# A Winograd down-projection in fp32 on one core: four PSUM banks a unit instead of seven, input and weight tiles split in two, operand loads on another queue

## The chip, the core and the metric

The kernel runs on one NeuronCore of a Trainium2 chip. It is one launch that computes a whole encoder layer for two sequences. The metric is the device time of the launch in microseconds (us). Engines are named as the profile names them: PE (TensorE, matmuls), DVE (VectorE), ACT (ScalarE), POOL (GpSimd) and SP (SyncE, which here only issues DMAs). Each engine carries out its own instructions in the order in which they stand in its program, and waits where one of them needs something that another engine or a DMA has not finished.

## The reference, cut to what matters

```python
def encoder_layer(x, ...):                       # x: (1, L, 1024); L = 2048 ("s") and L = 512 ("p")
    ...                                          # three mixers side by side, output projection
    x = x + cat @ w_out
    h = rms_norm(x, norm2_g)
    u = dwconv3(h @ w_ffn_in, ffn_conv_w, ffn_conv_b)          # 1024 -> 2 * 2816, then a width-3 convolution
    act = jax.nn.gelu(u[..., :D_FF], approximate=False) * u[..., D_FF:]
    return x + act @ w_ffn_out                                 # 2816 -> 1024: the down-projection
```

Everything is fp32. The change concerns the last line, `x + act @ w_ffn_out`, and one queue in the line with `w_ffn_in`.

## The kernel before

Every product is formed from three matmuls (`mm3`, lines 326 to 328): an operand is split into a rounded part and a rest (`split`, ACT copies the rounded part on line 320, DVE or POOL subtracts it on line 321), and high x high, high x low and low x high are added up in one PSUM bank.

The layer runs in stages. The mixers and the first quarter of the up-projection take the first half of the span. Then `ffn_in7` computes the remaining up-projection as 2 x 2 blocks by Winograd's form of Strassen's scheme, with seven products instead of eight; its right-hand operands are seven sums of the transposed rows, prepared earlier in DRAM (`ops`) and fetched by `ffn_operands` (tiles `st`, loaded on line 1351; two buffers; split into the tiles `o`). It loads the up-projection's weights as tiles `fw` on SP's queue, and POOL forms their sums `fs` (lines 1398 to 1402). Its results, the activations, go to DRAM as `acts` and `actp`.

The last stage is the down-projection, `ffn_out`. It cuts the 2560 rows into ten units of 256 (eight of the long sequence, two of the short one) and the 2816 inner columns into eleven pairs of 128-blocks. Three passes take four, four and three pairs, and each pass goes over all ten units, adding its sum to a partial result that it loads from DRAM and stores again (`x2`, then `part0`, `part1`, then the output). For each unit and pair, four 128 x 128 blocks of activations (A11 to A22) and four 128 x 512 blocks of weights (B11 to B22) make one Winograd step with seven products:

- `out_weights` loads the pair's weights into `b` (line 1495, one buffer, 1 MB), forms four differences `t` on DVE (line 1500) and splits the seven operands into one tile `w` (five buffers: four pairs of a pass and one of the next).
- `out_input` loads a unit's four blocks into `a` (lines 1517 and 1518, two buffers, SP's queue), forms four sums on DVE (line 1521) and splits all seven operands with one instruction on ACT and one on DVE into one tile `ah` (three buffers).
- `ffn_out` adds each of the seven products up over the pass's pairs in a bank of its own, 21 matmuls a pair. A unit so holds seven of the eight banks, and the next unit begins in the eighth and goes on in banks as they are read. At a unit's end one ACT copy (line 1556: `p1`, tile `s0`) and seven DVE adds (line 1554) read the banks: `u2` (tile `s1`), `u3` (tile `s2`), and five adds into the four quarters of `x`. Four adds on POOL finish `x`, and POOL issues the store of `x` (line 1568) and the load of the next unit's `x` (line 1544). `x` has one buffer, so that load waits for the store.

At a unit's end the banks are combined like this:

```python
nc.scalar.activation(p1, ps[0], AF.Copy)
add(u2, ps[1], p1)
add(u3, ps[2], u2)
add(x12, ps[3], x12)
add(x22, ps[3], x22)
add(x11, ps[4], x11)
add(x21, ps[5], x21)
add(x12, ps[6], x12)
```

The order on each engine is not the order of the code: a scheduler places the instructions by its own estimate of when each can start, and tile buffers are reused as their last readers finish. What the engines carry out is therefore read from the built program.

## Time and profile before

| what | value |
|---|---|
| time, median of 3 runs | 3182.96 us (3179.11 to 3183.93) |
| the profiled execution's own time | 3188.23 us |
| its span, first to last instruction | 3186.5 us |
| mean granted PE clock | 0.973 |
| busy: PE, DVE, ACT, POOL | 2932.5, 2307.0, 1382.2, 810.8 us |
| down-projection, from the up-projection's last matmul to the end | 2495.8 to 3186.5 us |
| its matmuls | 3 x 770 |

The profile is one execution. A row of a group gives the line, engine, operation, output<-input, count, busy time and mean duration, then the idle time of the engine just before these instructions and what ended it. A row of the timeline gives start, duration and the instruction, with the wait before it in square brackets. A row of the waits gives who waited for whom, the total, how often and the longest. Busy matmuls overlap in this profile (each shows about 0.4 us where one is issued every 0.23 us), so PE's pace is read from counts. Line numbers are those of the kernel before.

### The profile page before, as it was taken

What the parts mean: (1) busy time and instruction counts of PE and PEld (TensorE: products, weight loads), DVE (VectorE), ACT (ScalarE), POOL (GpSimd) and SP (SyncE); (2) the same over time, 40 slices, a digit from 0 to 9 for tenths busy, and PEclk for the clock granted to TensorE, in tenths of its full rate; (3) what the DMA queues carried; (4) which work ended last, traced back from release to release, by engine and by line L of the source; (5) the groups of instructions that cost most, each with busy time, mean ns of one, the idle gap of its engine ahead of it and who ended that gap; (6) DMA issues with size and microseconds to landing.
All of it is one profiled execution on the core that took longest, in us unless ns stands there. A gap on an engine that the chain in (4) does not pass through costs nothing.

```text
span 3186.5 us, 41534 instructions
## 1 busy us (share of the span) xinstructions
PE 2932.5 (92%) x15134; PEld 2412.1 (76%) x15134; DVE 2307.0 (72%) x3792; ACT 1382.2 (43%) x2259; POOL 810.8 (25%) x626
## 2 busy tenths in 40 slices
PE   7999999999999989999789999899999798799887
PEld 6887888888888777777568888678888576577665
DVE  7443577769998768766478888877777777877775
ACT  5222444458876448543344444444444421321211
POOL 1000000012233231003154444433333033223243
PEclk9999999999999999999889999999999899899998
DMA  5555576653433465675642222322222343443444
GB/s 176 147 151 144 159 222 183 179 165 114 133 106 95 154 184 163 175 203 184 197 140 80 80 80 80 126 80 83 83 80 80 119 168 127 167 156 130 157 147 144
DMA packets 450338, 441.25 MB, mean 138 GB/s; under 512 B 76553, under 2 KB 380041, under 8 KB 447317
## 3 DMA queue, kind: packets, MB, share of 16 engines
q1 hardware_dynamic: 420709, 341.16, 36.5%
q0 software_dynamic: 19200, 73.41, 6.3%
q10 hardware_dynamic: 10224, 24.03, 1.9%
q8 instruction: 119, 1.95, 0.3%
q14 instruction: 86, 0.70, 0.1%
HBM read 313.73 MB, written 124.78 MB: 138 GB/s over the span
## 4 chain that ended last, share of the span: by engine, by line
PE 28%; DVE 9%; DMA 7%; POOL 3%; issue 2%; ACT 1%; SPq 0%; DVEq 0%; ACTq 0%; POOLq 0%
PE b L326 9%; PE b L328 9%; PE b L327 9%; DVE a L1521 3%; DVE ah L321 2%; DMA a<-acts 2%; DVE x L1554 2%; POOL x L1554 2%; DMA x<-part1s 1%; DMA out_dram<-x 1%; DVE w L321 1%; DMA a<-actp 1%; POOL o L321 1%; ACT ah L320 1%; DMA fw<-in_w_ffn_in_dram 1%
## 5 line engine op out<-in xcount | busy, mean ns | idle before, releaser
L326 PE MATMUL b<-o,fk 128*128 128x512 f32 x1056 | 423.6, 401 | 16.8 <-ACT fk L320 13.2
L327 PE MATMUL b<-o,fk 128*128 128x512 f32 x1056 | 417.1, 395 | 5.1 <-DVE o L321 4.2
L328 PE MATMUL b<-o,fk 128*128 128x512 f32 x1056 | 418.6, 396 | 2.7 <-DVE fk L321 2.7
L326 PE MATMUL b<-w,ah 128*128 128x512 f32 x770 | 320.5, 418 | 92.1 <-DVE s L1554 41.7
L327 PE MATMUL b<-w,ah 128*128 128x512 f32 x770 | 312.3, 406 | 0.7 <-DVE w L321 0.5
L328 PE MATMUL b<-w,ah 128*128 128x512 f32 x770 | 311.8, 406 | 0.4 <-DVE ah L321 0.4
L1446 DVE SCALAR_TENSOR_TENSOR cv<-u,cst,cv 128x1024 f32<-128x1024 f32 (+2 forms) x264 | 298.9, 1173 | 7.9 <-ACT cv L1444 3.8
L320 ACT ACTIVATE ah<-a 128x896 fp32r<-128x896 f32 x110 | 104.1, 951 | 425.1 <-DVE a L1521 392.9
L326 PEld LDWEIGHTS b<-w,ah 128*128 128x128 f32 x770 | 149.1, 194 | 159.1 <-DVE s L1554 58.7
L1554 POOL TENSOR_TENSOR x<-x,s 128x512 f32<-128x512 f32 x120 | 174.7, 1481 | 349.1 <-DVE x L1554 349.1
L1521 DVE TENSOR_TENSOR a<-a 128x128 f32<-128x128 f32 x440 | 176.8, 428 | 107.0 <-DMA a<-acts 76.1
L326 PEld LDWEIGHTS b<-o,fk 128*128 128x128 f32 x1056 | 199.6, 189 | 63.8 <-ACT fk L320 13.6
L328 PEld LDWEIGHTS b<-o,fk 128*128 128x128 f32 x1056 | 199.7, 189 | 55.6 <-DVE fk L321 3.9
L327 PEld LDWEIGHTS b<-o,fk 128*128 128x128 f32 x1056 | 199.9, 189 | 53.5 <-DVE o L321 4.6
L1409 DVE TENSOR_TENSOR u<-b,u 128x512 f32<-128x512 f32 x220 | 151.3, 688 | 122.2 <-PE b L328 119.9
L326 PE MATMUL b<-W,h 128*128 128x256 f32 (+1 forms) x672 | 225.3, 335 | 2.2 <-ACT W L320 0.9
L349 POOL TENSOR_TENSOR rr<-ss,mhalf 128x1 f32<-128x1 f32 x60 | 37.1, 618 | 746.5 <-DVE ss L347 709.8
L1398 POOL TENSOR_TENSOR fs<-fw 128x512 f32<-128x512 f32 x44 | 94.0, 2136 | 513.1 <-DMA fw<-in_w_ffn_in_dram 418.3
L327 PE MATMUL b<-W,h 128*128 128x256 f32 (+1 forms) x672 | 215.1, 320 | 0.7 <-DVE pu L973 0.3
L328 PE MATMUL b<-W,h 128*128 128x256 f32 (+1 forms) x672 | 214.0, 318 | 0.0
L326 PE MATMUL b<-h,W 128*128 128x256 f32 x640 | 200.2, 313 | 3.6 <-ACT W L320 1.7
L328 PE MATMUL b<-h,W 128*128 128x256 f32 x640 | 184.9, 289 | 3.7 <-DVE W L321 3.7
(249 smaller groups left out, 7366.4 us busy)
## 6 DMA issues: line engine op xcount, KB each, us to landing
fw<-in_w_ffn_in_dram SPq DMA_DIRECT2D x132, 512.0 KB, 3.9
a<-acts SPq DMA_DIRECT2D x176, 128.0 KB, 2.6
nx<-in_x_sample_dram SPq DMA_DIRECT2D x32, 512.0 KB, 4.5
tf<-in_t2f_s_dram SPq DMA_DIRECT2D x64, 256.0 KB, 3.7
ops<-o SPq DMA_DIRECT2D x8, 1792.0 KB, 8.7
st<-ops SPq DMA_DIRECT2D x14, 1024.0 KB, 5.4
raw<-in_w_in_dram SPq DMA_DIRECT2D x44, 256.0 KB, 3.0
acts<-cv ACTq DMA_DIRECT2D x22, 512.0 KB, 4.3
```

The source lines that it names most:

```text
L320: self.keep(nc.scalar.activation(hi, x, AF.Copy))
L321: self.keep((engine or nc.vector).tensor_tensor(lo, x, hi.bitcast(F32), op=ALU.subtract))
L326: nc.tensor.matmul(ps, lhsT=lhi, rhs=rhi, start=start, stop=False, skip_group_check=more)
L327: nc.tensor.matmul(ps, lhsT=lhi, rhs=rlo, start=False, stop=False, skip_group_check=more)
L328: nc.tensor.matmul(ps, lhsT=llo, rhs=rhi, start=False, stop=stop, skip_group_check=more)
L349: self.keep(nc.gpsimd.tensor_tensor(r[:n], ss[:n], self.mhalf[:n, 0:1], op=ALU.pow))
L1398: nc.gpsimd.tensor_tensor(s12[:, 0:4], a21, a22, op=ALU.add)
L1409: nc.vector.tensor_tensor(o, ps, x, op=ALU.add)
L1446: nc.vector.scalar_tensor_tensor(o, u[:, part, c + i - 1:c + i - 1 + k], self.fcw[:, i, m:m + 1], o, op0=ALU.mult, op1=ALU.add)
L1521: nc.vector.tensor_tensor(a[:, o], a[:, x], a[:, y], op=op)
L1554: engine.tensor_tensor(o, a, b, op=ALU.add)
```

## The change

Four of the seven products get a bank: `pa`, `pb`, `pd` and `pc`. They are formed pair by pair as before (12 matmuls a pair, "early" products). When all pairs of the unit are done, `pa` is copied, `pb` and `pd` are added into `u2` and `u3`, and `pc` is added into `x22`. Then `pa`, `pd` and `pc` are not started afresh: another product ("late" product, all pairs of the unit one after the other) is accumulated on top of what the bank holds, and the sum is added into `x11`, `x21` and `x12`. A unit holds four banks, two units all eight. One bank add on DVE and one add on POOL fall away in each unit.

The late products need their operands after the early ones of all pairs, so the tiles are cut in two: inputs `ah` (four operands, two buffers) and `ag` (three operands, five buffers), each with its own split; weights `w` (four operands, five buffers) and `v` (three operands, four buffers), with five splits a pair instead of four. `a` gets a third buffer. The next pass's weights are written in the code after the last late product of the last unit, no longer between its pairs. Apart from the down-projection, `ffn_operands` issues the seven `st` loads of its first call on POOL's queue; those of the second call stay on SP's.

```diff
-    def ffn_operands(self, pool, stage, src):
+    def ffn_operands(self, pool, stage, src, queue):
...
-                self.nc.sync.dma_start(out=x, in_=src[:, op])
+                queue.dma_start(out=x, in_=src[:, op])
...
     def out_weights(self, pool, stage, f0):
-        w = pool.tile([128, 2, 7, 512], F32R, tag="w", bufs=5, name="w")
...
+        w = pool.tile([128, 2, 4, 512], F32R, tag="w", bufs=5, name="w")
         self.split(b11, w[:, 0, 0], w[:, 1, 0])
         less(t[:, 0], b12, b11)
         less(t[:, 1], b22, t[:, 0])
-        self.split(t[:, 0:2], w[:, 0, 3:5], w[:, 1, 3:5])
         less(t[:, 2], t[:, 1], b11)
+        self.split(t[:, 1:3], w[:, 0, 2:4], w[:, 1, 2:4])
+        self.split(t[:, 0], w[:, 0, 1], w[:, 1, 1])
+        v = pool.tile([128, 2, 3, 512], F32R, tag="v", bufs=4, name="v")
         less(t[:, 3], b21, t[:, 1])
-        self.split(t[:, 2:4], w[:, 0, 5:7], w[:, 1, 5:7])
-        self.split(b[:, 1].rearrange("p (h d) -> p h d", h=2), w[:, 0, 1:3], w[:, 1, 1:3])
-        return w
+        self.split(b[:, 1].rearrange("p (h d) -> p h d", h=2), v[:, 0, 0:2], v[:, 1, 0:2])
+        self.split(t[:, 3], v[:, 0, 2], v[:, 1, 2])
+        return w, v
 
     def out_input(self, pool, n, r0, f0):
-        a = pool.tile([128, 8, 128], F32, tag="a", bufs=2, name="a")
+        a = pool.tile([128, 8, 128], F32, tag="a", bufs=3, name="a")
...
-        h = pool.tile([128, 2, 7, 128], F32R, tag="ah", bufs=3, name="ah")
-        self.split(a[:, 0:7], h[:, 0], h[:, 1])
-        return h
+        h = pool.tile([128, 2, 4, 128], F32R, tag="ah", bufs=2, name="ah")
+        g = pool.tile([128, 2, 3, 128], F32R, tag="ag", bufs=5, name="ag")
+        self.split(a[:, 0:4], h[:, 0], h[:, 1])
+        self.split(a[:, 4:7], g[:, 0], g[:, 1])
+        return h, g
...
-                ps = [bank() for _ in order]
+                pa, pb, pd, pc = (bank() for _ in range(4))
...
-                    for p, (ja, jb) in zip(ps, order):
-                        self.mm3(p, h[:, 0, ja], h[:, 1, ja], ws[k][:, 0, jb], ws[k][:, 1, jb], k == 0, k == len(fs) - 1)
-                    if u == len(units) - 1 and i + 1 < len(passes):
-                        for g in passes[i + 1][len(nxt):k + 2]:
-                            nxt.append(self.out_weights(pw, stage, g))
+                    w = ws[k][0]
+                    for p, ja, jb in ((pa, 0, 0), (pb, 2, 2), (pd, 3, 3), (pc, 1, 1)):
+                        self.mm3(p, h[:, 0, ja], h[:, 1, ja], w[:, 0, jb], w[:, 1, jb], k == 0, k == len(fs) - 1)
...
+                def late(p, ja, jb):
+                    for k, g in enumerate(gs):
+                        v = ws[k][1]
+                        self.mm3(p, g[:, 0, ja], g[:, 1, ja], v[:, 0, jb], v[:, 1, jb], False, k == len(gs) - 1, True)
+
+                nc.scalar.activation(p1, pa, AF.Copy)
+                add(u2, pb, p1)
+                add(u3, pd, u2)
+                add(x22, pc, x22)
+                late(pa, 1, 0)
+                add(x11, pa, x11)
+                late(pd, 2, 2)
+                add(x21, pd, x21)
+                late(pc, 0, 1)
+                if u == len(units) - 1:
+                    for g in ahead:
+                        nxt.append(self.out_weights(pw, stage, g))
+                add(x12, pc, x12)
                 add(x22, x22, u3, nc.gpsimd)
-                add(x11, x11, p1, nc.gpsimd)
-                add(x21, x21, u3, nc.gpsimd)
-                add(x12, x12, u2, nc.gpsimd)
+                for o in (x21, x12):
+                    add(o, o, u2, nc.gpsimd)
```

What stands on DVE in a steady unit of the first pass, before. `s1` and `s2` are `u2` and `u3`; `b0` to `b4` are banks; the three `a` and `ah` that follow belong to the next two units:

```order
L1554 TENSOR_TENSOR s2_22752<-b0_22619,s1_22751 128x512
L1554 TENSOR_TENSOR x_22665<-b1_22620,x_22665 128x512 x2
L1554 TENSOR_TENSOR x_22665<-b2_22621,x_22665 128x512
L1554 TENSOR_TENSOR x_22665<-b3_22622,x_22665 128x512
L1554 TENSOR_TENSOR x_22665<-b4_22623,x_22665 128x512
L321 TENSOR_TENSOR ah_22807<-a_22804,ah_22807 128x896
L1521 TENSOR_TENSOR a_22837<-a_22837 128x128 x4
L321 TENSOR_TENSOR ah_22840<-a_22837,ah_22840 128x896
```

And in the change, from the add of `pc` (bank `b3`) into `x22` on. `a_22828`, `a_22855` and `a_22880` are the second, third and fourth inputs of the next unit, `a_22959` is the first of the one after it:

```order
L1558 TENSOR_TENSOR x_22685<-b3_22646,x_22685 128x512
L1522 TENSOR_TENSOR a_22880<-a_22880 128x128 x4
L1558 TENSOR_TENSOR x_22685<-b0_22643,x_22685 128x512
L1558 TENSOR_TENSOR x_22685<-b2_22645,x_22685 128x512
L321 TENSOR_TENSOR ag_22836<-a_22828,ag_22836 128x384
L321 TENSOR_TENSOR ag_22863<-a_22855,ag_22863 128x384
L321 TENSOR_TENSOR ag_22888<-a_22880,ag_22888 128x384
L1558 TENSOR_TENSOR x_22685<-b3_22646,x_22685 128x512
L1522 TENSOR_TENSOR a_22959<-a_22959 128x128 x4
L321 TENSOR_TENSOR ag_22967<-a_22959,ag_22967 128x384
L321 TENSOR_TENSOR ah_22862<-a_22855,ah_22862 128x512
```

The bank adds no longer stand together: input sums and splits stand between them, and the `ah` split of the next unit's third input comes after the sums of an input one unit later.

What stands on DVE at the end of the first pass, before. `w_23714` belongs to the second pair of the next pass (its differences stand far ahead of here), `b_23764` to the third:

```order
L321 TENSOR_TENSOR w_23714<-b_23715,w_23714 128x512
L1521 TENSOR_TENSOR a_23880<-a_23880 128x128
L321 TENSOR_TENSOR w_23714<-t_23717,w_23714 128x1024 x2
L321 TENSOR_TENSOR w_23714<-b_23715,w_23714 128x1024
L321 TENSOR_TENSOR ah_23829<-a_23826,ah_23829 128x896
L1521 TENSOR_TENSOR a_23880<-a_23880 128x128 x2
L321 TENSOR_TENSOR ah_23883<-a_23880,ah_23883 128x896
L1500 TENSOR_TENSOR t_23766<-b_23764 128x512
```

And in the change. `v_23899` is the second tile of the next pass's first pair, whose `w` tile is written in the pass's first units; `b_23905` is the second pair, `x_23777` the last unit:

```order
L1558 TENSOR_TENSOR x_23777<-b6_23737,x_23777 128x512
L321 TENSOR_TENSOR v_23899<-b_23886,v_23899 128x1024
L321 TENSOR_TENSOR v_23899<-t_23888,v_23899 128x512
L1558 TENSOR_TENSOR x_23777<-b7_23738,x_23777 128x512
L321 TENSOR_TENSOR ag_24004<-a_23996,ag_24004 128x384
L321 TENSOR_TENSOR ag_24031<-a_24023,ag_24031 128x384
L321 TENSOR_TENSOR ag_24056<-a_24048,ag_24056 128x384
L321 TENSOR_TENSOR ah_24030<-a_24023,ah_24030 128x512
L1499 TENSOR_TENSOR t_23907<-b_23905 128x512
```

The first pair's second half now stands among the last unit's adds, and the second pair's whole preparation behind them.

What stands on DVE at the end of a unit of the third pass, before:

```order
L1554 TENSOR_TENSOR s2_26341<-b7_26239,s1_26340 128x512
L1554 TENSOR_TENSOR x_26285<-b0_26240,x_26285 128x512 x2
L1554 TENSOR_TENSOR x_26285<-b1_26241,x_26285 128x512
L1554 TENSOR_TENSOR x_26285<-b2_26242,x_26285 128x512
L1554 TENSOR_TENSOR x_26285<-b3_26243,x_26285 128x512
```

And in the change:

```order
L1558 TENSOR_TENSOR x_26358<-b3_26319,x_26358 128x512
L1558 TENSOR_TENSOR x_26358<-b0_26316,x_26358 128x512
L1558 TENSOR_TENSOR x_26358<-b2_26318,x_26358 128x512
L321 TENSOR_TENSOR ah_26571<-a_26564,ah_26571 128x512
L321 TENSOR_TENSOR ag_26502<-a_26494,ag_26502 128x384
L1558 TENSOR_TENSOR x_26358<-b3_26319,x_26358 128x512
```

Two splits stand between the third and the fourth add into `x`; on PE the late product into `b3` stands between early products of the next unit.

More of the change, by code (lines that the diff above doesn't have):

```diff
@@ L1504, in out_weights @@
         less(t[:, 1], b22, t[:, 0])
-        self.split(t[:, 0:2], w[:, 0, 3:5], w[:, 1, 3:5])
         less(t[:, 2], t[:, 1], b11)
+        self.split(t[:, 1:3], w[:, 0, 2:4], w[:, 1, 2:4])
+        self.split(t[:, 0], w[:, 0, 1], w[:, 1, 1])
+        v = pool.tile([128, 2, 3, 512], F32R, tag="v", bufs=4, name="v")
         less(t[:, 3], b21, t[:, 1])
-        self.split(t[:, 2:4], w[:, 0, 5:7], w[:, 1, 5:7])
-        self.split(b[:, 1].rearrange("p (h d) -> p h d", h=2), w[:, 0, 1:3], w[:, 1, 1:3])
-        return w
+        self.split(b[:, 1].rearrange("p (h d) -> p h d", h=2), v[:, 0, 0:2], v[:, 1, 0:2])
+        self.split(t[:, 3], v[:, 0, 2], v[:, 1, 2])
+        return w, v
     def out_input(self, pool, n, r0, f0):
         nc = self.nc
-        a = pool.tile([128, 8, 128], F32, tag="a", bufs=2, name="a")
+        a = pool.tile([128, 8, 128], F32, tag="a", bufs=3, name="a")
         src = self.act[n][f0 * 128:f0 * 128 + 256, r0:r0 + 256].rearrange("(j p) (i t) -> j p i t", p=128, i=2)
         nc.sync.dma_start(out=a[:, 0:8:7], in_=src[0])
-        nc.sync.dma_start(out=a[:, 1:3], in_=src[1])
-        h = pool.tile([128, 2, 7, 128], F32R, tag="ah", bufs=3, name="ah")
-        for o, x, y, op in ((3, 7, 2, ALU.add), (4, 3, 0, ALU.subtract), (5, 0, 7, ALU.subtract), (6, 1, 4, ALU.subtract)):
+        nc.sync.dma_start(out=a[:, 5:7], in_=src[1])
+        for o, x, y, op in ((1, 7, 6, ALU.add), (2, 1, 0, ALU.subtract), (3, 0, 7, ALU.subtract), (4, 5, 2, ALU.subtract)):
             nc.vector.tensor_tensor(a[:, o], a[:, x], a[:, y], op=op)
-        self.split(a[:, 0:7], h[:, 0], h[:, 1])
-        return h
+        h = pool.tile([128, 2, 4, 128], F32R, tag="ah", bufs=2, name="ah")
[3 more added lines that the diff above has]
+        return h, g
     def ffn_out(self, units, passes, pool, stage, pw):
@@ L1530, in ffn_out @@
                 + [self.d["y_" + s.name][0]] for s in SEQS.values()}
-        order = ((0, 0), (4, 4), (5, 5), (3, 3), (1, 1), (2, 6), (6, 2))
         ws = [self.out_weights(pw, stage, passes[0][0])]
@@ L1535, in ffn_out @@
             nxt = []
+            ahead = list(passes[i + 1]) if i + 1 < len(passes) else []
             for u, (n, r0) in enumerate(units):
-                ps = [bank() for _ in order]
+                pa, pb, pd, pc = (bank() for _ in range(4))
+                gs = []
                 for k, f in enumerate(fs):
@@ L1540, in ffn_out @@
                         ws.append(self.out_weights(pw, stage, fs[k + 1]))
-                    h = self.out_input(pool, n, r0, f)
+                    h, g = self.out_input(pool, n, r0, f)
+                    gs.append(g)
                     if k == 1:
@@ L1554, in add @@
                     engine.tensor_tensor(o, a, b, op=ALU.add)
-                nc.scalar.activation(p1, ps[0], AF.Copy)
-                add(u2, ps[1], p1)
-                add(u3, ps[2], u2)
-                add(x12, ps[3], x12)
-                add(x22, ps[3], x22)
-                add(x11, ps[4], x11)
-                add(x21, ps[5], x21)
-                add(x12, ps[6], x12)
+                def late(p, ja, jb):
[15 more added lines that the diff above has]
+                add(x12, pc, x12)
                 add(x22, x22, u3, nc.gpsimd)
-                add(x11, x11, p1, nc.gpsimd)
-                add(x21, x21, u3, nc.gpsimd)
-                add(x12, x12, u2, nc.gpsimd)
+                for o in (x21, x12):
+                    add(o, o, u2, nc.gpsimd)
                 nc.gpsimd.dma_start(out=part[n][i + 1][r0:r0 + 256, :].rearrange("(i p) d -> p i d", p=128), in_=x)
@@ L1686, in run @@
             for i, parts in enumerate(([(S, 512, 1024)], [(S, 1536, 512), (P, 0, 512)])):
-                self.drive(self.ffn_in7(pool, *self.ffn_operands(hops, stage, self.ops[i]), parts, fb, last), None, 0)
+                self.drive(self.ffn_in7(pool, *self.ffn_operands(hops, stage, self.ops[i], nc.sync if i else nc.gpsimd), parts, fb, last), None, 0)
             for out, x in last:
```

## The prediction

> **What bounds the kernel now.** I looked first at the stretches by engine. The down-projection begins where the up-projection's last matmul ends, at 2495.8 us, and its three passes over the columns end at 2740.3, 2979.9 and, with the last store, 3186.5.
>
> ```profile
> 2100.00:2200.00 100.00, 100.00 (x431) 80.42 (x430) 74.17 (x110) 48.57 (x66) 29.17 (x20) 1.00 0.28 86
> ...
> 2495.80:2740.30 244.50, 212.01 (x843) 159.97 (x843) 189.14 (x321) 66.48 (x76) 65.94 (x54) 0.94 0.43 147
> 2740.30:2979.90 239.60, 207.76 (x840) 159.73 (x840) 180.84 (x303) 58.46 (x68) 73.93 (x60) 0.94 0.44 149
> 2979.90:3186.50 206.60, 160.84 (x628) 121.92 (x627) 140.18 (x229) 35.41 (x43) 77.88 (x65) 0.91 0.43 145
> ```
>
> The columns are PE, PEld, DVE, ACT, POOL, each with its count, then the granted clock. Before the stage PE issues 431 matmuls in 100 us, one in 0.232. The stage's 2310 would then take 536 us and take 690.7, so up to 155 us are PE waiting, DVE being busy for 510 of the 690.7. The waits say on what:
>
> ```profile
> PE b L326 <- DVE s L1554: 41.7, 25, 5.4
> PE b L326 <- ACT ah L320: 30.0, 5, 13.0
> PE b L326 <- DVE x L1554: 13.3, 20, 2.0
> DVE a L1521 <- DMA a<-acts: 76.1, 43, 4.3
> ```
>
> The rows on `s` and `x` are banks that PE wants and the vector engine has not read; `ah` is the split input. The stores that close the units (first and last of steady runs, and of the kernel) give the pace:
>
> ```profile
> 2551.41 0.74 POOL L1568 DMA_DIRECT2D part0s<-x  x1 [0.30 <-POOL x L1554]
> ...
> 2728.84 0.74 POOL L1568 DMA_DIRECT2D part0p<-x  x1 [0.30 <-POOL x L1554]
> ...
> 2788.55 0.74 POOL L1568 DMA_DIRECT2D part1s<-x  x1 [0.30 <-POOL x L1554]
> ...
> 2968.58 0.74 POOL L1568 DMA_DIRECT2D part1p<-x  x1 [0.30 <-POOL x L1554]
> ...
> 3015.58 0.74 POOL L1568 DMA_DIRECT2D out_dram<-x  x1 [0.30 <-POOL x L1554]
> ...
> 3180.32 0.74 POOL L1568 DMA_DIRECT2D out_dram<-x  x1 [0.30 <-POOL x L1554]
> ```
>
> Eight units take 177.4 us in pass one (22.2 each) and 180.0 in pass two (22.5), where 84 matmuls need 19.5; nine take 164.7 in pass three (18.3), where 63 need 14.6. The rest is lost at the starts of passes: 2728.8 to 2788.6 is 59.8 us for two units.
>
> **A steady unit of passes one and two.** These rows are one unit's vector work, with POOL's adds beside it:
>
> ```profile
> 2628.74 1.20 DVE L1521 TENSOR_TENSOR a<-a 128x128 f32<-128x128 f32 x4 [2.89 <-DMA a<-acts]
> 2629.86 1.08 DVE L321 TENSOR_TENSOR ah<-a,ah 128x896 fp32r<-128x896 f32 x1
> ...
> 2632.26 3.07 DVE L1554 TENSOR_TENSOR x<-b,x 128x512 f32<-128x512 f32 x5
> 2635.25 1.86 DVE L321 TENSOR_TENSOR ah<-a,ah 128x896 fp32r<-128x896 f32 x1
> ```
> ```profile
> 2633.63 5.94 POOL L1554 TENSOR_TENSOR x<-x,s 128x512 f32<-128x512 f32 x4 [10.05 <-DVE x L1554]
> ```
> ```profile
> 2658.89 3.21 DVE L1521 TENSOR_TENSOR a<-a 128x128 f32<-128x128 f32 x4
> ```
>
> An input costs 1.2 + 1.1 us on DVE when POOL is idle; under POOL's adds (1.5 each) a split takes 1.86 and four small adds 3.2, while adds that read a bank keep 0.61. The change drops one bank add and one POOL add a unit and cuts each split in two, 512 and 384 columns. The second half costs a fixed part: 0.69 for 512 and 1.22 for 1024 (below) leave about 0.16 an instruction, so 4 x 0.16 = +0.6 against -0.6. DVE's load stays level, near the 16.1 us a unit of these eight (128.47 / 8), under PE's 19.5.
>
> ```profile
> 2788.60:2968.60 180.00, 165.99 (x687) 127.97 (x686) 128.47 (x224) 38.78 (x45) 59.20 (x49) 0.99 0.42 142
> ```
>
> What goes is the bank wait: early products of the next unit write the four other banks, read a unit ago. What is late next is the input. In the changed order on DVE the split `ag` of the next unit's second input stands behind the add of `x21`, which waits for the second late product; that split frees the buffer for the load of the first input of the unit after next; and its four adds and `ag` stand ahead of the `ah` split that PE needs for the next unit's third input. From the second late product's end PE has the third late product and two inputs' early products ahead, 12 + 24 matmuls, 8.4 us. The chain in it: add of `x21` 0.8 with its semaphore, `ag` 0.8 under POOL, load 3.0 (2.6 to landing, 0.4 to issue), four adds 1.2 to 1.7, ACT's `ag` and `ah` 1.2.
>
> ```profile
> a<-acts SPq DMA_DIRECT2D x172, 128.0 KB, 2.6
> b<-in_w_ffn_out_dram SPq DMA_DIRECT2D x10, 1024.0 KB, 5.1
> ...
> x<-part1s POOLq DMA_DIRECT2D x8, 1024.0 KB, 5.3
> ```
> ```profile
> L320 ACT ACTIVATE w<-b 128x512 fp32r<-128x512 f32 x11 | 7.0, 632 | 35.3 <-DMA b<-in_w_ffn_out_dram 21.1 <-PE b L328 9.9 <-DVE a L1521 4.4
> ```
>
> Sum 7.0 to 7.5 of 8.4, so PE does not wait and a unit takes 19.5 to 19.8. At the far end, load 5.1 with its issue (the longest wait above is 4.3), adds 3.2, splits under POOL, it is 11 to 12 and a unit takes 22 to 23. I take 19.7, since no `x` transfer runs when that load does.
>
> The Trainium skill, "SBUF — State Buffer", section "Who interferes with whom", has a two-SBUF-input VectorE instruction and a GpSimd read exclude one another for a whole instruction, while one with a single SBUF input is untouched. The trace agrees in kind (1.08 against 1.86, bank adds unchanged); by that rule `ag` could wait out a POOL add, and the chain would be 8.2 of 8.4, an estimate that leaves the sum and adds to the slower rival's chance.
>
> **Pass starts.** Weights of a pair cost a load and nine vector instructions:
>
> ```profile
> 2743.21 0.69 DVE L321 TENSOR_TENSOR w<-b,w 128x512 fp32r<-128x512 f32 x1
> ...
> 2744.42 1.22 DVE L321 TENSOR_TENSOR w<-b,w 128x1024 fp32r<-128x1024 f32 x1
> ...
> 2753.28 1.40 DVE L1500 TENSOR_TENSOR t<-b 128x512 f32<-128x512 f32 x1 [0.56 <-DMA b<-in_w_ffn_out_dram]
> ```
> ```profile
> 2765.14 0.79 PE L326 MATMUL b<-w,ah 128*128 128x512 f32 x1 [9.78 <-ACT ah L320]
> ...
> 2768.14 0.63 PE L326 MATMUL b<-w,ah 128*128 128x512 f32 x1
> 2768.57 0.63 PE L327 MATMUL b<-w,ah 128*128 128x512 f32 x1
> ...
> 2770.70 0.53 PE L326 MATMUL b<-w,ah 128*128 128x512 f32 x1
> ```
>
> ```profile
> 2495.80:2551.40 55.60, 37.27 (x122) 25.62 (x123) 48.50 (x80) 24.10 (x27) 6.06 (x4) 0.79 0.34 114
> ```
>
> First pass: the four pairs and seven inputs take DVE until about 2547 in both kernels (it is busy 48.5 of these 55.6 us). By then PE has issued more before (122 by 2551.4) than it can after, where only 72 are free: three early inputs, one of the next unit, the fourth, one late product. The other two late products wait for adds; with 25 matmuls (5.8) and some 2 us for the adds, 97 are done at 2555. Left are 743 x 0.232 = 172.4, plus 2: the pass ends at 2729.5 instead of 2740.3, **-11**.
>
> Second pass. With its end of pass one as T: the next pair's `v` part has no free buffer (four, all in use) until the last unit's late products read it at T - 2. Its source `b`, a single buffer, is held with it, so the second pair's load cannot be issued before T + 0.3. Before, that pair lay staged. Three pairs follow one another, 5.1 to land and about 5 until `b` is read (four subtractions, three splits), then 2 for the last splits: about T + 33, T + 38 at seven us of reading. PE has 72 matmuls done then, and restarts slowly: after 9.8 us of idling it issues one in 0.43 until 2770.7. The 25 that follow, partly at that pace, and the adds between them take 9: first unit complete at T + 42; 743 more and 2 make T + 216.4, against 239.6 now: **-23**.
>
> The Trainium skill, "TensorE: Matmul & The Clock Gate", Part 1, says the array idles at half clock and needs one busy window of about 3.4 us to come back; by that a restart loses 1.7 us, an estimate, where these rows show 5.6 us at half pace, a loss of 2.6. The measured one counts.
>
> Third pass. `x` keeps one buffer, and its round sets the pace:
>
> ```profile
> 3039.26 0.72 POOL L1544 DMA_DIRECT2D x<-part1s  x1 [4.23 <-DMA out_dram<-x]
> ...
> 3052.28 0.74 POOL L1568 DMA_DIRECT2D out_dram<-x  x1 [0.30 <-POOL x L1554]
> ```
> ```profile
> 3044.67 3.08 DVE L1554 TENSOR_TENSOR x<-b,x 128x512 f32<-128x512 f32 x5 [0.92 <-DMA x<-part1s]
> ```
>
> From landing to store it is 7.6: two adds, then POOL's four. After the change it is the add of `x22` 0.7, nine matmuls of the last late product 2.3, beside them two adds and two splits until 3.7, the add of `x12` 0.6, POOL's last add 1.5 and 0.3: 6.2, at contended splits 7.4. So 18.3 - 1.4 = 16.9; I take 17.0, ends 16.5 and 18.3. The first unit ends 30.5 after the pass begins (two pairs' weights, 21, then 9.5), nine rounds 153, the last store to the end 6.2 as now: 189.7 against 206.6, **-17**.
>
> **The operand loads on POOL's queue.** The first seven `st` loads leave SP, where they wait for buffers ahead of `fw`, and queue among POOL's splits and sums.
>
> ```profile
> PE b L326 <- ACT fk L320: 13.2, 1, 13.2
> ```
> ```profile
> L321 POOL TENSOR_TENSOR o<-st,o x6: 4524/4631/6562, 1583.9 to 2068.5; 128x2048 fp32r<-128x2048 f32 x6
> ```
>
> `fw` comes up to 6 us sooner, which shortens the 13.2; the third load comes one POOL split (4.6) later. I take 0, from -6 to +5.
>
> **The sum.** -11 - 23 - 17 = -51 against the profiled execution's 3188.23 (span 3186.5): 3137. The median of the runs is 5.3 below that execution, so **3132**.
>
> **The rivals.** (a) Forecast, 0.60. (b) Inputs set the pace of passes one and two at 21.0: 17 units beside the first ones x 1.3 = +22, 3154; for it, DVE waits 76 us for `a` now; against, a third buffer. 0.15. (c) Pass starts cost 12 us more each, as `b` is read for seven us: two changes, +24, 3156. For it, T + 38 above; 0.10. (d) Both: 3178, no change; 0.04. (e) `x`'s round at 16.5, units at 19.5, `fw` early: -5 -3 -6, 3118; 0.04. (f) Slower: the chain through `ag`, load and `ah` takes the far end and beyond, 12.1 instead of 8.4, so each unit 23.2: 17 x 3.7 = +63, 3195. It outweighs the gains above 11.4 (51 / 17 = 3.0 over 8.4). Against it, the load starts outside `x`'s transfers. 0.07.
>
> Faster by over 0.2% (6.4 us, about what can be told from no change): a, b, c, e, 0.89; same 0.04; slower 0.07. Range 3113 to 3168: (e) with the 2.6 of a slow restart gone at both changes of pass, and (c) with `x`'s round at its upper end, 9 x 1.3 = 12 more.
>
> **What would show it.** Right: stores 19.5 to 20 us apart in the first two passes and about 17 in the third; hardly a PE wait on `s` or `x` there; `b` landing 5 us after each pass's end; the first store later than 2551. Wrong: steady stores over 21 apart with PE waiting on `ah`; third-pass stores still 18.3 apart; a change of pass over 60 us.

## The result and the profile after

The changed kernel takes 3155.11 us (median of 4 runs, 3153.54 to 3156.92) where the kernel before takes 3183.44 (4 runs, 3179.11 to 3185.67): a ratio of 0.9913, 95% interval 0.9896 to 0.9930, or 28.3 us less. The profiled execution took 3153.54 (span 3151.7) against 3188.23 (span 3186.5) before. Line numbers from here on are those of the changed kernel: adds on 1558, the copy `p1` on 1565, inputs on 1519 to 1522, weight loads on 1494.

The stretches by pass after the change, each from the end of the pass before it, and a stretch of steady units, from the second to the ninth store of the second pass (columns as before):

```profile
2492.00:2728.10 236.10, 211.22 (x842) 161.51 (x842) 189.15 (x367) 73.09 (x122) 53.71 (x47) 0.92 0.45 148
2728.10:2952.60 224.50, 207.72 (x842) 159.58 (x841) 177.46 (x337) 65.88 (x112) 56.94 (x51) 0.95 0.48 159
2952.60:3151.70 199.10, 161.77 (x631) 122.60 (x629) 129.54 (x242) 44.74 (x77) 60.53 (x53) 0.92 0.46 156
2795.00:2936.50 141.50, 141.41 (x600) 111.39 (x599) 108.37 (x211) 35.88 (x63) 39.98 (x35) 1.00 0.47 156
```

The passes took 244.5, 239.6 and 206.6 us before and take 236.1, 224.5 and 199.1 now. In the steady stretch PE is busy for all but 0.1 of 141.5 us and issues a matmul in 0.236: there the bound has become PE. DVE is busy for 108.4 of them, 15.5 a unit.

What PE waits for in the stage, after:

```profile
PE b L326 <- ACT w L320: 28.6, 6, 9.8
PE b L326 <- DVE x L1558: 23.7, 11, 7.1
PE b L327 <- DVE w L321: 7.7, 7, 1.3
PE b L326 <- DVE s L1558: 4.0, 6, 1.1
PE b L326 <- ACT ah L320: 3.6, 4, 1.3
```

The wait on `s`, 41.7 before, is 4.0. New in first place is `w`: the early weights at the three pass starts. The waits on `x` are 4.7 in the first two passes and 19.0 in the third, 7.1 of it in the last unit. The stores, first and ninth of each pass and the last one:

```profile
2552.49 0.75 POOL L1581 DMA_DIRECT2D part0s<-x  x1 [0.30 <-POOL x L1558]
...
2712.03 0.75 POOL L1581 DMA_DIRECT2D part0p<-x  x1 [0.30 <-POOL x L1558]
...
2774.26 0.75 POOL L1581 DMA_DIRECT2D part1s<-x  x1 [0.30 <-POOL x L1558]
...
2936.51 0.75 POOL L1581 DMA_DIRECT2D part1p<-x  x1 [0.30 <-POOL x L1558]
...
2987.31 0.75 POOL L1581 DMA_DIRECT2D out_dram<-x  x1 [0.30 <-POOL x L1558]
...
3145.61 0.75 POOL L1581 DMA_DIRECT2D out_dram<-x  x1 [0.30 <-POOL x L1558]
```

From such stores every kernel of this study can be laid out in the same seven pieces, in us: "start" is from the up-projection's last matmul (its start) to the first store; a unit is the mean distance of stores one to nine in passes one and two, and one to ten in pass three; a "change" runs from the ninth store of a pass to the first of the next, two units; "stage" is from that last matmul to the end of the span. The 6 us behind the last store are in the stage alone.

| kernel | start | unit, pass 1 | change 1 | unit, pass 2 | change 2 | unit, pass 3 | stage |
|---|---|---|---|---|---|---|---|
| before | 56.0 | 22.2 | 59.7 | 22.5 | 47.0 | 18.3 | 691.1 |
| after | 60.9 | 19.9 | 62.2 | 20.3 | 50.8 | 17.6 | 660.1 |
| E1 two b | 55.8 | 20.3 | 56.8 | 20.3 | 44.7 | 18.1 | 651.1 |
| E2 two x | 60.9 | 19.9 | 63.6 | 19.5 | 50.0 | 17.2 | 650.3 |
| E3 five v | 60.8 | 19.9 | 53.5 | 20.0 | 41.2 | 18.3 | 645.5 |
| E4 no banks | 57.4 | 22.2 | 52.9 | 23.0 | 45.6 | 19.0 | 694.2 |
| E5 queue on SP | 60.6 | 20.0 | 62.1 | 19.8 | 50.8 | 17.6 | 656.6 |
| E6 two a | 60.1 | 20.3 | 66.6 | 20.4 | 50.8 | 18.1 | 672.4 |
| E7 four a | 59.1 | 20.2 | 64.2 | 20.4 | 50.1 | 17.6 | 663.5 |
| E8 two x, four a | 60.7 | 19.8 | 63.1 | 19.6 | 50.9 | 17.0 | 649.7 |
| E9 eight ag, four w | 60.2 | 21.7 | 65.4 | 21.4 | 52.2 | 17.1 | 683.0 |
| E10 two x, eight ag, four w | 60.0 | 20.4 | 65.3 | 20.0 | 52.7 | 16.9 | 659.0 |
| E11 as E10, five v | 60.2 | 20.4 | 58.0 | 20.0 | 45.1 | 17.0 | 645.4 |
| E12 two x, two b, five v, four w | 55.6 | 20.0 | 54.5 | 19.8 | 43.1 | 17.7 | 636.9 |

Between before and after the 16 steady units of the first two passes give 8 x 2.24 + 8 x 2.22 = 35.7 us and the third pass 6.4. The start takes back 4.9, the changes 2.5 and 3.8. That leaves 31 of the stage; the other 3.8 of the spans' 34.8 lie ahead of it (E5). E5 has the same instructions in the stage as the changed kernel, and its stage is 3.5 shorter: so much can be scatter in one row of this table.

### The profile page after: what moved, and what is told of

Read it like the earlier page. It is cut to its first block, busy times and chain, and to the rows that moved or that the text cites. A ratio compares the mean times of both kernels' runs of the same rounds, so it can differ in the third digit from the quotient of the medians.

```text
span 3151.7 us, 41678 instructions
## 1 busy us (share of the span) xinstructions
PE 2933.1 (93%) x15134; PEld 2414.2 (77%) x15134; DVE 2291.3 (73%) x3883; ACT 1404.7 (45%) x2380; POOL 766.3 (24%) x603
## 4 chain that ended last, share of the span: by engine, by line
PE 31%; DMA 8%; DVE 6%; POOL 2%; issue 2%; ACT 1%; SPq 0%; POOLq 0%; DVEq 0%; ACTq 0%
PE b L327 10%; PE b L326 10%; PE b L328 10%; DMA out_dram<-x 1%; DVE x L1558 1%; DVE ag L321 1%; DMA x<-part1s 1%; DVE a L1522 1%; DMA x<-x2s 1%; DMA fw<-in_w_ffn_in_dram 1%; POOL x L1558 1%; DMA part0s<-x 1%; DMA b<-in_w_ffn_out_dram 1%; POOL o L321 1%; DVE t L1499 0%
## 5 line engine op out<-in xcount | busy, mean ns | idle before, releaser
L326 PEld LDWEIGHTS b<-o,fk 128*128 128x128 f32 x1056 | 200.7, 190 | 65.3 <-ACT fk L320 11.6
L1558 POOL TENSOR_TENSOR x<-x,s 128x512 f32<-128x512 f32 x90 | 128.0, 1427 | 360.5 <-DVE x L1558 248.3
L326 PE MATMUL b<-w,ah 128*128 128x512 f32 x440 | 181.8, 417 | 32.3 <-ACT w L320 28.6
L1522 DVE TENSOR_TENSOR a<-a 128x128 f32<-128x128 f32 x440 | 153.2, 369 | 68.8 <-DMA a<-acts 46.7
L326 PE MATMUL b<-h,W 128*128 128x256 f32 x640 | 200.3, 313 | 2.9 <-ACT o L487 1.0
L327 PE MATMUL b<-w,ah 128*128 128x512 f32 x440 | 183.0, 416 | 8.0 <-DVE w L321 7.7
L328 PE MATMUL b<-h,W 128*128 128x256 f32 x640 | 184.9, 289 | 4.0 <-DVE W L321 4.0
L320 ACT ACTIVATE fk<-fs 128x1024 fp32r<-128x1024 f32 x88 | 91.5, 1059 | 209.5 <-PE b L328 90.1
L327 PE MATMUL b<-h,W 128*128 128x256 f32 x640 | 183.1, 286 | 0.0
L328 PE MATMUL b<-w,ah 128*128 128x512 f32 x440 | 181.3, 414 | 0.8 <-DVE ah L321 0.8
```

The lines of the kernel that those rows point to most:

```text
L320: self.keep(nc.scalar.activation(hi, x, AF.Copy))
L326: nc.tensor.matmul(ps, lhsT=lhi, rhs=rhi, start=start, stop=False, skip_group_check=more)
L327: nc.tensor.matmul(ps, lhsT=lhi, rhs=rlo, start=False, stop=False, skip_group_check=more)
L328: nc.tensor.matmul(ps, lhsT=llo, rhs=rhi, start=False, stop=stop, skip_group_check=more)
L1522: nc.vector.tensor_tensor(a[:, o], a[:, x], a[:, y], op=op)
L1558: engine.tensor_tensor(o, a, b, op=ALU.add)
```

## The experiments

Each kernel ran on the same chip as the kernel before, which took 3185.4 us beside E1 to E4, 3177.2 beside E5 to E8, 3180.5 beside E9 to E11 and 3175.3 beside E12. Kernels of different groups are therefore compared by their ratio to the kernel before; the changed kernel's is 0.9913 (0.9896 to 0.9930).

**E1, two buffers for b.** Edit of the changed kernel:

```diff
-        b = stage.tile([128, 2, DM], F32, tag="b", name="b")
+        b = stage.tile([128, 2, DM], F32, tag="b", bufs=2, name="b")
```

> The changed kernel with a second buffer for b, the raw rows of a weight pair, so that a pair's load no longer waits until the pair before it has been read. Theory (the vector engine sets the pace of a pass's start): in the changed kernel pairs come 11.7 and 10.1 us apart, of which the vector engine is busy about 9.6 (7.3 for the pair's nine instructions, 2.3 for an input); only its waits of 0.7 to 1.2 us for b and what hangs on them go, 1.5 to 2 a pair, eight pairs, so 10 to 15 us less: 3140 to 3145. Rival (the loads set it, 5.1 us each): the whole load comes off each of the eight spacings, 25 us or more: 3130 or below. If b is held by v's buffers in any case, no change: 3155.

Measured: 3145.84 us, 0.9880 (0.9866 to 0.9893). When DVE begins on a pair at the first change of pass, in the changed kernel and then in E1:

```profile
2734.46 0.69 DVE L1499 TENSOR_TENSOR t<-b 128x512 f32<-128x512 f32 x1 [0.90 <-DMA b<-in_w_ffn_out_dram]
...
2746.12 0.69 DVE L1499 TENSOR_TENSOR t<-b 128x512 f32<-128x512 f32 x1 [1.23 <-DMA b<-in_w_ffn_out_dram]
...
2756.30 0.69 DVE L1499 TENSOR_TENSOR t<-b 128x512 f32<-128x512 f32 x1 [0.68 <-DMA b<-in_w_ffn_out_dram]
```
```profile
2728.89 0.68 DVE L1499 TENSOR_TENSOR t<-b 128x512 f32<-128x512 f32 x1
...
2736.98 0.68 DVE L1499 TENSOR_TENSOR t<-b 128x512 f32<-128x512 f32 x1
...
2746.20 0.69 DVE L1499 TENSOR_TENSOR t<-b 128x512 f32<-128x512 f32 x1
```

The spacing falls from 11.7 and 10.2 to 8.1 and 9.2, and no row of E1 waits for `b`: once the load is off the path, DVE's own row of instructions sets the pace, as the theory has it. Start and changes give 5.1, 5.4 and 6.1 us; about half of that is lost in the steady units of passes one and three.

**E2, two buffers for x.**

```diff
-                        x = pool.tile([128, 2, DM], F32, tag="x", name="x")
+                        x = pool.tile([128, 2, DM], F32, tag="x", bufs=2, name="x")
```

> The changed kernel with a second buffer for x, the tile of partial sums. Theory (x's round of load, adds, store is what sets the third pass, 17.6 us a unit, and the waits on x of 1.7 to 3.0 us in the second units of the first two passes): units of the third pass go to about 15.2, just above the 14.7 of 63 matmuls, nine times 2.4 is 21, and 4 more from the second units and 2 at the tail: about 3130. Rival (the vector engine, held up by the GpSimd adds, or the input loads that now share the engines with x's, take over in the third pass): units at 16.5, 10 us less in all: 3145.

Measured: 3148.50 us, 0.9883 (0.9870 to 0.9897). For the third pass the rival holds in kind: 17.2 a unit, not 15.2, and more than the 16.5 that it gave. DVE's waits there, from the second store to the ninth in the changed kernel (seven units) and from the third to the ninth in E2 (six), and the landing of inputs in the same stretches:

```profile
DVE a L1522 <- DMA a<-acts: 11.7, 7, 3.0
DVE x L1558 <- DMA x<-part1s: 11.1, 6, 2.4
...
DVE a L1522 <- DMA a<-actp: 5.3, 2, 3.5
```
```profile
DVE a L1522 <- DMA a<-acts: 20.3, 11, 2.4
DVE a L1522 <- DMA a<-actp: 11.1, 6, 2.2
```
```profile
a<-acts SPq DMA_DIRECT2D x24, 128.0 KB, 2.5
a<-actp SPq DMA_DIRECT2D x12, 128.0 KB, 2.3
```
```profile
a<-acts SPq DMA_DIRECT2D x20, 128.0 KB, 5.1
...
a<-actp SPq DMA_DIRECT2D x12, 128.0 KB, 5.0
```

The wait for `x` is gone, and the wait for inputs has grown from 17.0 in seven units (2.4 each) to 31.4 in six (5.2 each): a 128 KB load that landed in 2.5 us now takes 5, issued beside a 1 MB store and a 1 MB load of `x` (medians of the fourteen and twelve loads whose landing the traces have). The distances of the ten stores in E2's third pass say the same from another side: 13.6, 21.1, 17.7, 19.3, 17.5, 19.2, 17.8 and then 13.8 and 14.4, where 63 matmuls need 14.6. Behind 3110.6 us, in the last two units, no input is loaded any more. In the second pass, on the other hand, the theory holds: with no wait on `x` a unit takes 19.5, what 84 matmuls need. In the first it stays at 19.9.

**E3, five buffers for v.**

```diff
-        v = pool.tile([128, 2, 3, 512], F32R, tag="v", bufs=4, name="v")
+        v = pool.tile([128, 2, 3, 512], F32R, tag="v", bufs=5, name="v")
```

> The changed kernel with five buffers for the late weights v instead of four, so that one whole pair of the next pass can be staged and b is free for the next load before the pass ends. Theory (the held b costs the two changes of pass about one load each): the two units around the first change of pass take 62.2 us and around the second 50.8, where they took 59.7 and 47.0 before the change; with five buffers 5 us less at each, nothing at the first pass: 3145. Rival (the vector engine's instructions are all in a row and set the time): 0 to 2 us less: 3153 to 3155.

Measured: 3140.84 us, 0.9862 (0.9849 to 0.9876). The loads of `b` around the first change of pass, in the changed kernel (pass end 2728.1) and in E3:

```profile
2729.31 0.37 SPq L1494 DMA_DIRECT2D b<-in_w_ffn_out_dram  x1
...
2739.56 0.37 SPq L1494 DMA_DIRECT2D b<-in_w_ffn_out_dram  x1
...
2751.08 0.37 SPq L1494 DMA_DIRECT2D b<-in_w_ffn_out_dram  x1
```
```profile
2732.54 0.37 SPq L1494 DMA_DIRECT2D b<-in_w_ffn_out_dram  x1
...
2742.94 0.37 SPq L1494 DMA_DIRECT2D b<-in_w_ffn_out_dram  x1
...
2755.16 0.37 SPq L1494 DMA_DIRECT2D b<-in_w_ffn_out_dram  x1
```

Of the four pairs of the new pass three are loaded behind the pass end in the changed kernel. In E3 it is two, and the load at 2755.16 is a pair for later: DVE begins on pairs at 2737.85 and 2750.05 and not again until the first unit is through. The changes of pass take 8.7 and 9.6 us less, more than the 5 expected: a whole load with its reading goes. So the held `b` is the cause of what the changes of pass cost in the changed kernel, and with a fifth buffer they are shorter than before the change (53.5 and 41.2 against 59.7 and 47.0).

**E4, the change without the banks.** The kernel before, with two parts of the change:

```diff
-                self.nc.sync.dma_start(out=x, in_=src[:, op])
+                (self.nc.gpsimd if queue else self.nc.sync).dma_start(out=x, in_=src[:, op])
...
-        a = pool.tile([128, 8, 128], F32, tag="a", bufs=2, name="a")
+        a = pool.tile([128, 8, 128], F32, tag="a", bufs=3, name="a")
```

> The kernel before with two parts of the change alone: a third buffer for a, and the first seven operand loads on GpSimd's queue; seven banks, one weight tile and the old order stay. Theory (the four banks with their late products are what brings units from 22.3 to 20.1 us; the inputs are not what held it): the queue gives its 4 us, the third buffer at most 0.3 a unit: 3172 to 3180. Rival (the third buffer alone shortens the units, as the vector engine waited 76 us for a): units of 21, 17 times 1.3 and the 4 of the queue: about 3157.

Measured: 3190.28 us, 1.0014 (1.0005 to 1.0023): a trace slower than before, and outside both expectations on the slow side; of the rival's 25 us nothing came. What PE waits for in its stage (line numbers of before):

```profile
PE b L326 <- DVE s L1554: 34.2, 23, 3.1
PE b L326 <- DVE x L1554: 29.2, 18, 4.3
```

The bank waits of before are still there, 63 us where they were 55. Neither the third input buffer nor the queue shortens a unit as long as seven banks have to be read: what brings 22.3 down to 20.1 is the four banks with their late products and split tiles.

**E5, the operand loads back on SP's queue.**

```diff
-                self.drive(self.ffn_in7(pool, *self.ffn_operands(hops, stage, self.ops[i], nc.sync if i else nc.gpsimd), parts, fb, last), None, 0)
+                self.drive(self.ffn_in7(pool, *self.ffn_operands(hops, stage, self.ops[i], nc.sync), parts, fb, last), None, 0)
```

> The changed kernel with the first seven operand loads back on SP's queue. In the trace of the changed kernel the up-projection's last matmul starts at 2491.6, before the change at 2495.4, in the run without the four banks (loads on GpSimd's queue) at 2496.2, and at 2492 to 2494 in the changed kernel's variants. Theory (the queue is worth nothing and these differences are scatter): 3153 to 3157, with that last matmul anywhere from 2491 to 2496. Rival (the queue gives 3 to 4 us): 3158 to 3160 and the last matmul at 2495 or later.

Measured: 3143.24 us, 0.9899 (0.9882 to 0.9917); the interval overlaps the changed kernel's. The up-projection's last matmul in E5, and in E6, which has the queue of the change:

```profile
2486.43 0.40 PE L328 MATMUL b<-o,fk 128*128 128x512 f32 x1
```
```profile
2481.64 0.39 PE L328 MATMUL b<-o,fk 128*128 128x512 f32 x1
```

With nothing but buffers of the last stage different, that matmul comes at 2481.6 to 2494.5 in this study's profiles. The 3.8 us by which it came sooner in the changed kernel's profile lie within that scatter, which is wider than both expectations had it: with the loads on SP's queue the matmul came at 2486.4, earlier than either gave. The queue is worth nothing that these runs can show.

**E6, two buffers for a.**

```diff
-        a = pool.tile([128, 8, 128], F32, tag="a", bufs=3, name="a")
+        a = pool.tile([128, 8, 128], F32, tag="a", bufs=2, name="a")
```

> The changed kernel with two buffers for the input a, as before the change. Theory (the chain of the prediction: split, load, adds, split within what PE has ahead): with two buffers a load is issued one input later, 2.8 us of PE's 8.4 are lost and the chain of 7.0 to 7.5 no longer fits, so PE waits 1.4 to 2 us a unit; 27 units, 38 to 54 us: 3193 to 3209. Rival (the third buffer carries nothing, the loads are issued early enough): 3155 to 3160.

Measured: 3158.97 us, 0.9948 (0.9928 to 0.9967), some 11 us above the changed kernel by the ratios, whose intervals just touch, and 12 by the stage; on the same chip E5, whose stage is that of the changed kernel, ran in 3141.48 to 3148.59 us and E6 in 3155.75 to 3170.06. Neither expectation: the third buffer carries something, but between a fifth and a third of what the chain gave. PE does not come to wait on the split `ah` as that chain has it (3.4 us in the stage) but on the copy `p1` on ACT (9.3 us in 14 waits, 1.8 in 4 with three buffers). In the steady units of the first two passes a split of `ag` stands ahead of that copy and waits 2.7 to 5.9 us for DVE's sums of an input; such a place is shown at E9.

**E7, four buffers for a.**

```diff
-        a = pool.tile([128, 8, 128], F32, tag="a", bufs=3, name="a")
+        a = pool.tile([128, 8, 128], F32, tag="a", bufs=4, name="a")
```

> The changed kernel with four buffers for the input a. Theory (in the third pass the vector engine, which works in order, stands up to 3.5 us before an input that has not landed, and the adds into x stand behind it, so x's round is 17.6 instead of 17.0 or less): with one more input loaded ahead the waits for a of 17 us in seven units go, about 1 us a unit in the third pass and 0.3 in the others: 15 us less, 3140. Rival (x's round alone, of load, adds and store, sets the third pass): 0 to 3 us less, 3152 to 3155.

Measured: 3159.48 us, 0.9947 (0.9930 to 0.9964). The theory falls: not a microsecond less, but by the ratios some 11 us more and by the stage 3.4; the third pass stays at 17.6, and DVE's waits for inputs even grow (77.6 us in the stage against 62.4).

**E8, two x and four a.** The edits of E2 and E7 together.

```diff
-        a = pool.tile([128, 8, 128], F32, tag="a", bufs=3, name="a")
+        a = pool.tile([128, 8, 128], F32, tag="a", bufs=4, name="a")
...
-                        x = pool.tile([128, 2, DM], F32, tag="x", name="x")
+                        x = pool.tile([128, 2, DM], F32, tag="x", bufs=2, name="x")
```

> The changed kernel with two buffers for x and four for a. With two for x alone the third pass kept 17.5 us a unit, the input loads took 5.1 us to land instead of 2.5, beside the stores and loads of x, and the vector engine waited 31 us for them in six units. Theory (those late inputs are what took x's place): with one more input ahead the wait of 5 us a unit shrinks to under 2, units of the third pass go to 15.5, so 18 us less than the 3148.5 of two x alone: about 3130. Rival (the transfers or the adds on GpSimd set it, not the order of the loads): 3145 to 3149.

Measured: 3143.84 us, 0.9898 (0.9883 to 0.9913); the rival holds. Units of the third pass are 17.0 against E2's 17.2, and the middle ones 17.6 to 20.7. So it is not the number of input buffers that makes the inputs late.

**E9, eight buffers for ag.** To make room, `w` has four buffers.

```diff
-        w = pool.tile([128, 2, 4, 512], F32R, tag="w", bufs=5, name="w")
+        w = pool.tile([128, 2, 4, 512], F32R, tag="w", bufs=4, name="w")
...
-        g = pool.tile([128, 2, 3, 128], F32R, tag="ag", bufs=5, name="ag")
+        g = pool.tile([128, 2, 3, 128], F32R, tag="ag", bufs=8, name="ag")
```

> The changed kernel with eight buffers instead of five for the late half of an input, ag, and, to make room, four instead of five for the early weights w. In the run with two x and four a the split into ag waits for PE 29 us in five units of the third pass, three ag splits in a row as the last late product reads them; a frees only behind that split, so the loads go out in a bunch beside the store. Theory (ag's buffers and x's round are both at their limit in the third pass, so that with one x only the first two passes gain): units of the third pass 17 to 17.6, those of the others 19.6 to 19.8 instead of 20.1; 0.989 of the kernel before, some 8 us under the changed kernel's 0.991, if four w cost nothing. Rival (ag alone sets the third pass): units of 16 or less there, 0.985.

Measured: 3179.35 us, 0.9994 (0.9982 to 1.0006): nearly the whole gain of the change is gone. Neither theory saw it. PE's waits in the stage, and one unit's place in the timeline:

```profile
PE b L326 <- ACT w L320: 31.0, 7, 9.8
PE b L326 <- ACT s L1565: 29.4, 19, 4.1
PE b L326 <- DVE x L1558: 19.1, 11, 6.6
```
```profile
2618.66 0.52 ACT L320 ACTIVATE ag<-a 128x384 fp32r<-128x384 f32 x1 [5.23 <-DVE a L1522]
2619.09 0.61 ACT L320 ACTIVATE ah<-a 128x512 fp32r<-128x512 f32 x1
...
2619.61 0.58 ACT L1565 ACTIVATE s<-b 128x512 f32<-128x512 f32 x1
...
2620.24 0.50 PE L326 MATMUL b<-v,ag 128*128 128x512 f32 x1 [1.93 <-ACT s L1565]
```

With room for three more `ag`, the split of a later input stands on ACT ahead of this unit's copy `p1`. It waits 5.23 us for DVE's sums, which wait for the input's load, and `p1`, whose bank is full, waits behind it; then PE waits for the bank. In the changed kernel's steady units of the first two passes an `ah` split stands there instead, and `p1` follows it within 0.1 us. E10 and E11, with eight `ag` too, have E9's order and wait for that copy 15.3 and 13.8 us; E12, with five `ag` but four `w` as here, waits 0.2. So it is `ag`'s buffers and not `w`'s that bring the wait. Why the scheduler places the split there is not shown, and the number of `ag` buffers alone does not decide it: E6 has five and the same order.

**E10 and E11, two x with eight ag, then also five v.** E10 has the edits of E2 and E9; E11 has that of E3 too. The diff is that of E11; E10 lacks its second edit.

```diff
-        w = pool.tile([128, 2, 4, 512], F32R, tag="w", bufs=5, name="w")
+        w = pool.tile([128, 2, 4, 512], F32R, tag="w", bufs=4, name="w")
...
-        v = pool.tile([128, 2, 3, 512], F32R, tag="v", bufs=4, name="v")
+        v = pool.tile([128, 2, 3, 512], F32R, tag="v", bufs=5, name="v")
...
-        g = pool.tile([128, 2, 3, 128], F32R, tag="ag", bufs=5, name="ag")
+        g = pool.tile([128, 2, 3, 128], F32R, tag="ag", bufs=8, name="ag")
...
-                        x = pool.tile([128, 2, DM], F32, tag="x", name="x")
+                        x = pool.tile([128, 2, DM], F32, tag="x", bufs=2, name="x")
```

> The changed kernel with two buffers for x, eight for ag and four for w. With two x alone the ratio to the kernel before was 0.988 and units of the third pass 17.5. Theory (the ag splits that wait for the last late product are what took x's place): units of the third pass 15.0 to 15.5, near the 14.7 of 63 matmuls, 18 us less: 0.982, about 3127 where the kernel before takes 3183. Rival (it is the input loads' slowness beside the store and the load of x, 5.1 us to land, or the adds on GpSimd under which splits take 1.8 us): 17 or more, 0.987 to 0.988.

> As the run before it (two x, eight ag, four w), with five buffers for the late weights v too. Theory: the gain of five v at the two changes of pass, 8.7 and 9.7 us in its own run, adds to whatever that run gives: 15 to 18 us less than it, 0.977 if that run comes to 0.982. Rival (with four w instead of five the staged pair has no early buffer until the last unit's first input is through, and the gain goes): no more than 5 us less than it.

Measured: E10 3149.45 us, 0.9894 (0.9880 to 0.9907); E11 3138.88, 0.9860 (0.9844 to 0.9875). In E10 the rival holds: third-pass units of 14.1, 19.4, 17.5, 18.8, 17.4, 18.9, 17.6, 14.0, 14.1, and inputs that land in 4.9 us. Neither the splits nor the buffers but the time at which inputs land goes with the 17 us. E11 is 10.6 us below E10, short of the 15 to 18 expected and over the rival's 5: 7.3 and 7.6 come off the two changes of pass, with four `w` in place.

**E12, two x, two b, five v and four w.** The edits of E1, E2 and E3, and four buffers for `w`.

```diff
-        b = stage.tile([128, 2, DM], F32, tag="b", name="b")
+        b = stage.tile([128, 2, DM], F32, tag="b", bufs=2, name="b")
...
-        w = pool.tile([128, 2, 4, 512], F32R, tag="w", bufs=5, name="w")
+        w = pool.tile([128, 2, 4, 512], F32R, tag="w", bufs=4, name="w")
...
-        v = pool.tile([128, 2, 3, 512], F32R, tag="v", bufs=4, name="v")
+        v = pool.tile([128, 2, 3, 512], F32R, tag="v", bufs=5, name="v")
...
-                        x = pool.tile([128, 2, DM], F32, tag="x", name="x")
+                        x = pool.tile([128, 2, DM], F32, tag="x", bufs=2, name="x")
```

> The changed kernel with the three edits that each gave something: two buffers for x, two for b, five for v, and four for w to make room; a and ag as in the changed kernel. Theory (the places are different: v and b act at the pass starts, x in the steady units of the first two passes): units of the first two passes at 19.5 to 19.8, the spans of two units around the changes of pass at 53 and 40 instead of 62.2 and 50.8, the third pass still 17.3 to 17.5 in its middle, as its input loads land beside x's store and load (5.0 us instead of 2.5); 22 to 30 us under the changed kernel, 0.982 to 0.984. Rival (with four w the staged pair comes late, or the edits free the same microseconds): 0.986 as with five v alone.

Measured: 3133.15 us where the kernel before takes 3175.30, 0.9859 (0.9838 to 0.9880). By its stage, 636.9, it is the shortest of all, 23.2 below the changed kernel, as the theory has it; but its units, 20.0 and 19.8, and its changes, 54.5 and 43.1, each come a little longer than forecast, and by the ratio the rival's 0.986 holds: it cannot be told from E3 or E11. All three beat both kernels, with intervals that lie below the changed kernel's. The simplest of them is E3, one number.

## Why the prediction was right, and where it was too large

The direction and the range were right; the forecast was too large. Of 51 us some 28 came: the median, forecast at 3132, is 23 us later, and the profiled execution, forecast at 3137, 16.5 us. By its own steps:

- **A steady unit.** Forecast 19.7; measured 19.9 and 20.3. The bank wait is gone, as argued, and PE does not come to wait on the inputs (3.6 us on `ah` in the whole stage). The slower rivals that rest on the inputs, at 21.0 and at 23.2, did not come. What the step missed is the second unit of each of the first two passes: its `x` can only be loaded when the first unit's late store has landed, and PE waits 1.7 and 3.0 us and, behind the 3.0, runs eight matmuls at half pace. E2 takes that away and gives 19.5 in the second pass.

  A contended split, from the third pass's first unit, with POOL's adds going on at the first row and not at the second:

```profile
2983.20 1.64 DVE L321 TENSOR_TENSOR ag<-a,ag 128x384 fp32r<-128x384 f32 x1
...
2988.01 0.56 DVE L321 TENSOR_TENSOR ag<-a,ag 128x384 fp32r<-128x384 f32 x1
```

  The Trainium skill, "SBUF — State Buffer", section "Who interferes with whom", has such a split wait out a POOL read; the trace agrees in kind (1.64 us against 0.56), and the slower rival to which it added a chance did not come.
- **First pass, -11: measured -8.4.** The first unit was complete 56 us after the pass's start, three sooner than forecast; the nine others took 180.1 instead of 174.4. The two errors partly cancel.
- **Second pass, -23: measured -15.1.** The pass start was forecast nearly to the microsecond: `b` issued 1.2 us after the pass end T, the third pair's weights done at T + 34.9 (forecast T + 33 to T + 38), the first unit complete at T + 41.9 (forecast T + 42). E3 confirms the reason given, that `v`'s four buffers hold `b`. The step that failed is "743 more and 2": 182.6 us instead of 174.4. Five to six us of it lie in the second unit, behind `x` (3.0 of waiting and 1.6 of half pace), and nearly three in the last two, whose cause stays open.
- **Third pass, -17: measured -7.5.** Two terms were too small. The two pairs' weights took 25.3 us (2952.6 to 2977.9), not 21, as pairs came 11.7 apart, and the first store came at T + 34.8 instead of T + 30.5. Nine rounds took 158.3, not 153. One round of `x` in the middle of the pass:

```profile
3059.75 0.75 POOL L1581 DMA_DIRECT2D out_dram<-x  x1 [0.30 <-POOL x L1558]
...
3064.75 0.72 POOL L1550 DMA_DIRECT2D x<-part1s  x1 [4.25 <-DMA out_dram<-x]
...
3070.11 1.89 DVE L1558 TENSOR_TENSOR x<-b,x 128x512 f32<-128x512 f32 x3 [1.44 <-DMA x<-part1s]
...
3074.23 0.68 DVE L1558 TENSOR_TENSOR x<-b,x 128x512 f32<-128x512 f32 x1
```

  Store to load 5.0, load to the first add 5.4, add to the next store at 3076.82 6.7: 17.1, and six of the nine rounds are of 16.5 to 17.3, as forecast. The others are of 17.8 to 19.9 and make the difference. E2 shows that the round is not alone in this place: without it the inputs, which land in 5 us, hold the unit at nearly the same length. That the transfers of `x` slow them was not isolated by an edit; it is argued from the landing times (last section) and from the last two units, which run at 14 us. Nor is it shown that POOL's adds, beside which a split takes 1.6 us instead of 0.6, have no part in it.
- **The operand loads' queue, 0:** E5 and E4 bear it out. What remains between the profiled spans' 34.8 and the medians' 28.3 is scatter ahead of the stage and in single executions.
- **The sum.** The terms came to -51 and measured -31.0 in the stage: 2.6, 7.9 and 9.5 us lacking in the three passes. The rival of dearer pass starts named the right place, but starts were dear by 4 us at one change and not at the other, not 12.
- **The markers.** The first store did come later than 2551 and `b` landed 5 us after its issue, itself 1.2 us behind the pass's end. Third-pass stores came 17.6 apart, between the 17 of the one sign and the 18.3 of the other. "A change of pass over 60 us" was a bad marker: the forecast's own terms, a unit of 19.5 and a start of 42, make 61.5, and the change measured 62.2.

## What to carry to other kernels

When one tile is cut in two, ask for each half which buffer it holds back while it waits: here the late weights' fourth buffer held the raw rows of the next pair, and one more buffer gave half as much again as the whole change. More buffers are not always better where engines work in order, as a scheduler may put work for later, still waiting for its data, ahead of the instruction that frees a bank now (E9, E10); fewer buffers can bring the same order (E6), so the order has to be read from the trace. A resource that sets the pace may have a second one close behind it; double it alone, look at what ends the next wait, and expect less than the whole distance to the next bound.
